# Three of four merged chunks turned by DMA transposes instead of by the matmul engine, in a hybrid attention and FFN layer

## The chip, the core and the metric

The kernel runs on one core of one Trainium2 chip. The core has a matmul engine (TensorE, PE in the profile), a vector engine (VectorE, DVE), an activation engine (ScalarE, ACT), a general engine (GpSimd, POOL) and a queue engine (SyncE, SP), and 16 DMA engines that move data for all of them. The metric is the device time of one execution in microseconds (us). The time before is the median of three runs, 1339.09 us (1338.78 to 1348.87).

## The reference

One layer on 256 rows of 2048 float32 values: a norm, one input projection, three kinds of attention, each projected and weighted with a gate, an output projection and a residual, then a norm, a gated feed-forward part and a residual. What the change touches is the line that merges the three branches and multiplies the sum with `w_out`:

```python
merged = (gates[:, :, 0] * (flat(o_a) @ w_branch[:ea])
          + gates[:, :, 1] * (flat(o_b) @ w_branch[ea:eb])
          + gates[:, :, 2] * (flat(o_c) @ w_branch[eb:]))
x = x + merged @ w_out

h2 = rmsnorm(x, g_ffn)
gu = h2 @ w_gu
x = x + (jax.nn.silu(gu[..., :D_FF]) * gu[..., D_FF:]) @ w_down
```

## The kernel before

The 256 rows are two tiles of 128 (`NT` = 2), and columns go in chunks of 512 (`NB`). Each float32 operand of a product is split into a high part of fewer bits and a rest: `split` (line 107) casts on ScalarE and subtracts on VectorE. A product of two such operands is three matmuls of 128x128 by 512 (lines 172 to 174). Weights come in blocks of 512 KB, two steps of k each (128 rows of the weight): `weights` (line 122) loads a block with a DMA of SP's queue into one of four `w_raw` buffers, casts it into one of five `w_hi` buffers and subtracts into one of five `w_lo`. `project` (line 147) runs over k for one chunk of output columns, with two tiles of rows, so that a block feeds 12 matmuls.

Work that is not a projection is written as generators in two lists, `stages` and `slow_stages`. `project` calls the first generator of `stages` once for each k but the first, and the first of `slow_stages` for each even k but the first: here a call is one step. A generator that ends is taken off, and the same call goes on with the next.

The order on an engine is set by a planner that simulates the kernel and takes what is ready, in program order as far as it can. `keep_in_program_order` pins an instruction behind the one written before it on the same engine; those written later can still be taken first. Buffers of a pool are given out as they come free.

The merge stage (lines 931 to 951): for each of four chunks, three projections with `w_branch` over 4, 6 and 6 steps of k give 3 + 5 + 5 = 13 calls of `stages`. Gates come back from memory with DMAs of POOL's queue (line 941) into buffers `sc` of 2 KB for each partition, of which there are 12 (`scratch`), and VectorE multiplies and adds (lines 945 to 948) into `ms`. The sum has rows on partitions, but the product with `w_out` needs it turned. So `to_m` (line 931) turns each half of a chunk (128 rows by 512 columns) with four TensorE transposes into PSUM (`transpose4`, line 201), and `m.put` splits them into `m_hi` and `m_lo`. One call of the generator does one half.

After that, `w_out` is projected in four chunks of columns over 16 steps of k (line 978), each of which reads all of m: chunk c of the merge is read at k = 4c to 4c + 3. `keep_x1` adds x, squares it and starts the next norm. `ph1` is the group of pools on the left side of the core's memory that holds the attention's output; it is closed at line 951, between the merge and the first `w_out` column, and the pools of the next stage are opened in its place.

In the feed-forward part `to_a` (line 1021) already turns 20 half chunks by DMA: a copy on ScalarE takes the two 16-bit halves of each float32 value apart into two planes (line 1034), a DMA transpose of ScalarE's queue turns the planes (line 1038), and another copy puts the halves together again (line 1047).

Of the kernel before, what the change touches and what calls it, by code (L numbers as in the profile page):

```python
# [11 lines left out]
U16 = mybir.dt.uint16  # L12
# [6 lines left out]
P = 128  # L19
D = 2048  # L20
S = 256
NT = S // P
KT = D // P
# [6 lines left out]
NB = 512  # L30
# [25 lines left out]
def hybrid_block(ctx: ExitStack, tc: tile.TileContext, x, w_in, w_branch, w_out, w_gu, w_down, rel_bias,  # L56
                 onehot, extra, across, factors, out):
    nc = tc.nc
# [22 lines left out]
    def pool(stack, name, side, bufs=1):  # L81
        return stack.enter_context(tc.tile_pool(name=name, bufs=bufs, side=side, reuse_waits="tile"))

    h2_stack, ph1, pm, pgx = ExitStack(), ExitStack(), ExitStack(), ExitStack()
# [6 lines left out]
    def half_kb(dt=F32):  # L91

        return scratch.tile([P, NB], dt, name="sc")
# [3 lines left out]
    def banks():  # L97

        turn.reverse()
        return [acc.tile([P, NB], F32, name=turn[1]) for _ in range(2)]  # L100
# [21 lines left out]
    def weights(w, row0, k0, nk, col0, there=()):  # L122

        for i, c in enumerate(range(k0, nk, 2)):
            raw = there[i] if i < len(there) else raw_weights(w, row0, c, col0)[0]
            hi = wpool.tile([P, 2, NB], F32R, name="w_hi")
            lo = wpool.tile([P, 2, NB], F32R, name="w_lo")
            split(hi, lo, raw)
            for k in range(2):
                yield c + k, hi[:, k, :], lo[:, k, :]  # L130


    stages, slow_stages = [], []

    def advance(queue):
        while queue:
            try:
                next(queue[0])
                return
            except StopIteration:  # L140
                queue.pop(0)

    def finish_stages(queue):
        while queue:
            advance(queue)

    def project(acts, k0, w, row0, nk, col0, ps=None, done=0, there=(), last=1):


        ps = ps or banks()  # L150
        held = []
        for k, w_hi, w_lo in weights(w, row0, done, nk, col0, there):
            if k:
                advance(stages)
            if k % 2 == 0 and k:
                advance(slow_stages)
            held.append((k, w_hi, w_lo))
            if k < nk - last or k == nk - 1:
                for t in range(NT):
                    for kk, hi, lo in held:  # L160
                        product(ps[t], *acts.plain(t, k0 + kk), hi, lo, kk == 0, kk == nk - 1)
                held = []
        return ps
# [5 lines left out]
    def product(ps, ah, al, wh, wl, start=False, stop=False):  # L169
        how = dict(skip_group_check=True)  # L170
        wh, wl = woven(wh), woven(wl)
        nc.tensor.matmul(ps, ah, wh, start=start, stop=False, **how)  # L172
        nc.tensor.matmul(ps, ah, wl, start=False, stop=False, **how)  # L173
        nc.tensor.matmul(ps, al, wh, start=False, stop=stop, **how)  # L174
# [26 lines left out]
    def transpose4(src):  # L201

        pt = tr.tile([P, 4, P], F32, name="tr")
        for i in range(4):
            nc.tensor.transpose(pt[:, i, :], src[:, i * P:(i + 1) * P], ident)  # L205
        return pt
# [127 lines left out]
    def begin_pair(acts, w, colA, colB):  # L334

        b11, b12 = (quarter(acts, w, 0, col0) for col0 in (colA, colB))
        p11 = [parts(b) for b in b11]
        u = [gx.tile([P, 2, NB], F32, name="u") for _ in acts.wc]
        for a, b, d in zip(b11, b12, u):
            nc.vector.tensor_add(d, a, b)  # L340
        b21 = quarter(acts, w, 1, colA)
        return p11, b12, u, b21, [parts(b) for b in (u if w is w_gu else b21)]
# [87 lines left out]
    h = Columns(p1, "h", KT)  # L430
# [7 lines left out]
    def load_x(c, queue):  # L438
        xc = [half_kb() for _ in range(NT)]
        for t in range(NT):  # L440
            queue(xc[t], x[t * P:(t + 1) * P, c * NB:(c + 1) * NB])
        return xc
# [408 lines left out]
    def gate_col(c, b):  # L851
        return 3 * NH * HD + b * D + c * NB

    def pair_of(kind, what):
        if kind == "qk":
            return hs, w_in, what * NB, NH * HD + what * NB
        if kind == "gates":
            return hs, w_in, gate_col(*what[0]), gate_col(*what[1])
        if kind == "vv":
            return hs, w_in, V0 + what[0] * NB, V0 + what[1] * NB  # L860
        if kind == "vg":
            return hs, w_in, V0 + what[0] * NB, gate_col(*what[1])
# [16 lines left out]
    for (kind, what), after in zip(units, units[1:] + [(None, None)]):  # L879
# [9 lines left out]
        if kind in ("qk", "gates", "vv", "vg"):  # L889
            ps, ahead = project_pair(*pair_of(kind, what), ahead, nxt, others is in_turn)  # L890
            if others is in_turn:
                turn.reverse()
        else:
            ps = project(h, 0, w_in, 0, KT, V0 + what * NB if kind == "v" else gate_col(*what),
                         *((ps0, 4, there) if (kind, what) == ("v", 0) else ()))
# [32 lines left out]
    tc.keep_in_program_order(nc.scalar.preload_act_table_set("natural_log_exp_and_others"))  # L928
    m = Columns(pool(pm, "pm", "right"), "m", KT)

    def to_m(c, srcs):
        for t in range(NT):
            m.put(c, t, transpose4(srcs[t]))
            yield

    for c in range(4):
        ms = [half_kb() for _ in range(NT)]
        for b, (k0, nk) in enumerate(((0, H_A), (H_A, H_B), (H_A + H_B, H_C))):
            gt = [half_kb() for _ in range(NT)]
            for t in range(NT):  # L940
                nc.gpsimd.dma_start(gt[t], gate_mem[b, c, t])
            ps = project(o, k0, w_branch, k0 * P, nk, c * NB)
            for t in range(NT):
                if b == 0:
                    nc.vector.tensor_mul(ms[t], ps[t], gt[t])
                else:
                    nc.vector.tensor_mul(gt[t], ps[t], gt[t])
                    nc.vector.tensor_add(ms[t], ms[t], gt[t])
        stages.append(to_m(c, ms))
    finish_stages(stages)  # L950
    ph1.close()


# [14 lines left out]
    def keep_x1(c, ps, xc):  # L968
        for t in range(NT):
            nc.vector.tensor_add(xc[t], ps[t], xc[t])  # L970
            nc.gpsimd.dma_start(x1[t, :, c * NB:(c + 1) * NB], xc[t])
        squares(xc, ss2, c)
        stages.append(next_h(c, xc))

    gx = pool(h2_stack, "gx2", "left", 2)
    for c in range(4):
        xc = load_x(c, nc.gpsimd.dma_start)
        ps = project(m, 0, w_out, 0, KT, c * NB)
        if c == 3:
            ahead = begin_pair(h2, w_gu, 0, D_FF)  # L980
        keep_x1(c, ps, xc)
# [301 lines left out]
```

## Time and profile before

| | us |
|---|---|
| median of three runs | 1339.09 |
| the profiled execution, first to last instruction (span) | 1337.6 |
| TensorE busy | 1331.3 |
| VectorE busy | 1154.7 |
| ScalarE busy | 927.8 |
| merge stage on TensorE, first product of a branch to first product with m | 514.9 to 600.4 |
| first `w_out` column on TensorE | 600.4 to 622.0 |

The span is what the profile shows of one execution; a run's time holds some more around it. Of TensorE the profile models the ends of the matmuls, which are pipelined, so that durations overlap and "busy" is not the same as "at its peak": the distance between starts is what counts. A row of the timeline gives start, duration, engine, line, operation, what is written and read, shapes and count, and in brackets the idle time before it with what ended it. PEclk is the TensorE clock that was granted, 1.00 being full speed. The DMA share is the mean busy share of the 16 DMA engines.

### The profile page before, as it was taken

To read this page: it belongs to the slowest core of one execution; us is meant where nothing else is said; L and a number is where in the kernel's file an instruction comes from. 1 tells how busy PE (TensorE), PEld (TensorE's weight loads), DVE (VectorE), ACT (ScalarE), POOL (GpSimd) and SP (SyncE) were. 2 spreads that over 40 slices of the span, in tenths; PEclk is the share of its full clock that TensorE was granted. 3 is DMA by queue.
4 is the path that set the end of the run, shared out by engine and by line. 5 is a ranking of instruction groups with operands and counts; after the bars stand their busy time and mean duration, and the time that the engine had idled before them with its cause. 6 is when DMAs were issued, how large, how long until landed. Compare 5 with 4: busy or idle time off the path is not lost.

```text
span 1337.6 us, 17737 instructions
## 1 busy us (share of the span) xinstructions
PE 1331.3 (100%) x6255; PEld 1161.6 (87%) x6255; DVE 1154.7 (86%) x1232; ACT 927.8 (69%) x1183; POOL 127.2 (10%) x191
## 2 busy tenths in 40 slices
PE   9999999999999999999999999999999999999998
PEld 6888888888888888888888888888888888888887
DVE  7978898988888897876689999998889997998887
ACT  6786967788777776445567787777877776665563
POOL 1100010001110112100100000001000001001010
PEclk9999999999999999999999999999999999999999
DMA  9987877888788878877797989889899987789993
GB/s 360 307 284 246 263 211 254 258 269 228 261 268 282 286 228 292 305 233 225 236 332 261 273 248 275 235 262 307 280 290 276 265 227 256 248 270 303 275 270 96
DMA packets 118929, 352.61 MB, mean 264 GB/s; under 512 B 32768, under 2 KB 34488, under 8 KB 118840
## 3 DMA queue, kind: packets, MB, share of 16 engines
q1 hardware_dynamic: 77016, 277.45, 58.4%
q0 software_dynamic: 19408, 67.66, 21.4%
q10 hardware_dynamic: 22416, 6.36, 3.2%
q8 instruction: 49, 0.80, 0.2%
q14 instruction: 40, 0.33, 0.1%
HBM read 294.26 MB, written 14.70 MB: 231 GB/s over the span
## 4 chain that ended last, share of the span: by engine, by line
PE 98%; DMA 1%; DVE 0%; SPq 0%; issue 0%; ACT 0%; DVEq 0%
PE qs L172 12%; PE qs L173 12%; PE qs L174 12%; PE ps L173 12%; PE ps L174 12%; PE ps L172 12%; PE z L172 4%; PE z L174 4%; PE z L173 4%; PE v L172 2%; PE v L174 2%; PE v L173 2%; PE tr L174 1%; PE tr L172 1%; PE tr L173 1%; PE tr L205 1%
## 5 line engine op out<-in xcount | busy, mean ns | idle before, releaser
L108 DVE TENSOR_TENSOR w_lo<-w_raw,w_hi 128x1024 fp32r<-128x1024 f32 x310 | 376.3, 1221 | 73.5 <-ACT w_hi L108 72.0
L108 ACT CAST w_hi<-w_raw 128x1024 fp32r<-128x1024 f32 x310 | 322.2, 1048 | 129.0 <-PE qs L174 52.8
L108 ACT CAST w_hi<-g_raw 128x1024 fp32r<-128x1024 f32 x208 | 214.4, 1050 | 103.6 <-DVE g_raw L329 32.1
L108 DVE TENSOR_TENSOR w_lo<-g_raw,w_hi 128x1024 fp32r<-128x1024 f32 x208 | 248.0, 1221 | 19.5 <-ACT w_hi L108 17.0
L108 ACT CAST w_hi<-u 128x1024 fp32r<-128x1024 f32 x156 | 162.6, 1048 | 107.0 <-PE ps L174 22.4
L108 DVE TENSOR_TENSOR w_lo<-u,w_hi 128x1024 fp32r<-128x1024 f32 x156 | 188.9, 1223 | 43.0 <-ACT w_hi L108 38.3
L173 PE MATMUL qs<-w_lo,h_hi 128*128 128x512 f32 x348 | 132.6, 381 | 0.0
L174 PE MATMUL qs<-w_hi,h_lo 128*128 128x512 f32 x348 | 132.1, 379 | 0.0
L173 PE MATMUL ps<-w_lo,h_hi 128*128 128x512 f32 x336 | 128.0, 381 | 0.3 <-DVE w_lo L108 0.2
L174 PE MATMUL ps<-w_hi,h_lo 128*128 128x512 f32 x336 | 127.4, 380 | 0.1
L172 PE MATMUL qs<-w_hi,h_hi 128*128 128x512 f32 x348 | 127.4, 382 | 0.0
L172 PE MATMUL ps<-w_hi,h_hi 128*128 128x512 f32 x336 | 123.0, 382 | 0.0
L172 PEld LDWEIGHTS qs<-w_hi,h_hi 128*128 128x128 f32 x348 | 65.7, 189 | 9.5 <-ACT sc L324 0.3
L174 PEld LDWEIGHTS qs<-w_hi,h_lo 128*128 128x128 f32 x348 | 65.8, 189 | 9.2
L173 PEld LDWEIGHTS qs<-w_lo,h_hi 128*128 128x128 f32 x348 | 65.8, 189 | 9.2
L388 POOL DMA_DIRECT2D u<-g_raw x44 | 38.3, 869 | 356.7 <-DVE w_lo L108 311.7
L173 PEld LDWEIGHTS ps<-w_lo,h_hi 128*128 128x128 f32 x336 | 63.5, 189 | 9.9 <-DVE w_lo L108 1.2
L174 PEld LDWEIGHTS ps<-w_hi,h_lo 128*128 128x128 f32 x336 | 63.5, 189 | 9.9 <-DVE h_lo L108 1.1
L172 PEld LDWEIGHTS ps<-w_hi,h_hi 128*128 128x128 f32 x336 | 63.3, 189 | 9.0 <-ACT h_hi L108 0.3
L340 DVE TENSOR_TENSOR u<-g_raw 128x1024 f32<-128x1024 f32 x44 | 53.6, 1221 | 11.7 <-DMA g_raw<-in_w_gu 11.0
L329 DVE TENSOR_TENSOR u<-u,g_raw 128x1024 f32<-128x1024 f32 x44 | 51.9, 1219 | 0.0
L172 PE MATMUL v<-w_hi,h_hi 128*128 128x512 f32 x104 | 39.5, 380 | 0.0
(407 smaller groups left out, 2945.8 us busy)
## 6 DMA issues: line engine op xcount, KB each, us to landing
w_raw<-in_w_in SPq DMA_DIRECT2D x103, 512.0 KB, 6.9
g_raw<-in_w_in SPq DMA_DIRECT2D x88, 512.0 KB, 6.3
g_raw<-in_w_gu SPq DMA_DIRECT2D x88, 512.0 KB, 6.0
w_raw<-in_w_gu SPq DMA_DIRECT2D x88, 512.0 KB, 6.6
w_raw<-in_w_down SPq DMA_DIRECT2D x56, 512.0 KB, 4.8
u<-g_raw POOLq DMA_DIRECT2D x48, 512.0 KB, 6.8
w_raw<-in_w_branch SPq DMA_DIRECT2D x32, 512.0 KB, 5.2
w_raw<-in_w_out SPq DMA_DIRECT2D x32, 512.0 KB, 4.3
```

Of the source, the lines that this page charges most:

```text
L108: cast, rest = nc.scalar.copy(hi, src), nc.vector.tensor_sub(lo, src, hi.bitcast(F32))
L172: nc.tensor.matmul(ps, ah, wh, start=start, stop=False, **how)
L173: nc.tensor.matmul(ps, ah, wl, start=False, stop=False, **how)
L174: nc.tensor.matmul(ps, al, wh, start=False, stop=stop, **how)
L205: nc.tensor.transpose(pt[:, i, :], src[:, i * P:(i + 1) * P], ident)
L329: tc.keep_in_program_order(nc.vector.tensor_add(d, d, a))
L340: nc.vector.tensor_add(d, a, b)
L388: nc.gpsimd.dma_start(d, a, accum_op=ALU.add)
```

## The change

Chunks 0, 1 and 2 of the merge are no longer turned on TensorE. The new `to_m` does with each half what `to_a` does: a copy on ScalarE into two 16-bit planes (`apart`), a DMA transpose on ScalarE's queue (`send`), and a copy that joins the planes in a scratch buffer (`join`), from which `m.put` splits as before. All three are pinned. Counted in calls of the generator, the halves are copied at call 2 and 6, sent at 3 and 7, and joined at 12 and 15; it has 15 calls for a chunk. The planes lie in a new pool of two buffers for each of the two tiles.

Chunk 3 is turned on TensorE as before, but from `slow_stages`, one half each at k = 4 and k = 6 of the first `w_out` column. That column, with its load of x, is now written ahead of `finish_stages` and the closing of `ph1`, because chunk 2's joins (k = 3 and 6 of this column) and chunk 3's transposes are called within it.

```diff
@@ -928,10 +928,45 @@
     m = Columns(pool(pm, "pm", "right"), "m", KT)
 
+    planes1 = pool(ph1, "planes1", "left", 2)
+
+    def apart(src):
+        halves = planes1.tile([P, 2, NB], U16, name="halves")
+        tc.keep_in_program_order(nc.scalar.copy(halves, src.bitcast(U16).rearrange("p (n h) -> p h n", h=2)))
+        return halves
+
+    def send(halves):
+        turned = planes1.tile([P, 8, P], U16, name="turned")
+        tc.keep_in_program_order(nc.scalar.dma_start_transpose(turned, halves.rearrange("p h n -> p (h n)")))
+        return turned
+
+    def join(turned):
+        st = half_kb()
+        tc.keep_in_program_order(nc.scalar.copy(
+            st.bitcast(U16).rearrange("p (k q h) -> p h k q", k=4, h=2),
+            turned.rearrange("p (h k) q -> p h k q", h=2)))
+        return st.rearrange("p (k q) -> p k q", k=4)
+
+    def steps(n):
+        for _ in range(n):
+            yield
+
     def to_m(c, srcs):
+        turned = []
         for t in range(NT):
+            yield from steps(2 * t + 1)
+            halves = apart(srcs[t])
+            yield
+            turned.append(send(halves))
+        yield from steps(5)
+        for t in range(NT):
+            m.put(c, t, join(turned[t]))
+            yield from steps(3 if t == 0 else 1)
+
+    def to_m_by_products(c, srcs):
+        for t in range(NT):
+            yield
             m.put(c, t, transpose4(srcs[t]))
-            yield
 
...
-        stages.append(to_m(c, ms))
+        if c < 3:
+            stages.append(to_m(c, ms))
+        else:
+            slow_stages.append(to_m_by_products(c, ms))
+    xc = load_x(0, nc.gpsimd.dma_start)
+    ps = project(m, 0, w_out, 0, KT, 0)
     finish_stages(stages)
+    finish_stages(slow_stages)
     ph1.close()
 
...
     for c in range(4):
-        xc = load_x(c, nc.gpsimd.dma_start)
-        ps = project(m, 0, w_out, 0, KT, c * NB)
+        if c:
+            xc = load_x(c, nc.gpsimd.dma_start)
+            ps = project(m, 0, w_out, 0, KT, c * NB)
```

## The prediction

> **What bounds the kernel now.** I read the page first (busy shares, the chain that ended last), then TensorE's waits, then the order of time around the merge stage (about 520 to 622 us), then the busy time in stretches of it.
>
> ```profile
> span 1337.6 us, 17737 instructions
> ...
> PE 1331.3 (100%) x6255; PEld 1161.6 (87%) x6255; DVE 1154.7 (86%) x1232; ACT 927.8 (69%) x1183; POOL 127.2 (10%) x191
> ...
> PE 98%; DMA 1%; DVE 0%; SPq 0%; issue 0%; ACT 0%; DVEq 0%
> ```
>
> ```profile
> PE tr L421 <- DVE sc L435: 1.1, 1, 1.1
> PE ps L526 <- DVE w_lo L520: 0.6, 1, 0.6
> PE ps L173 <- DVE w_lo L108: 0.2, 1, 0.2
> ```
>
> TensorE carries 98% of the chain that ended last. The second view gives who it waited for, with us in total, times and longest: 1.9 us in all, at three places. So the end moves only if TensorE gets less work, or if a new wait reaches it. The stage that the change touches, in stretches:
>
> ```profile
> core 0: us, PE busy (x) PEld busy (x) DVE busy (x) ACT busy (x) POOL busy (x), PEclk, DMA share, GB/s
> 541.00:550.00 9.00, 9.00 (x47) 7.95 (x46) 7.71 (x10) 4.23 (x5) 1.71 (x4) 1.00 0.94 330
> 550.00:562.00 12.00, 12.00 (x58) 10.50 (x57) 10.37 (x14) 5.25 (x5) 2.16 (x4) 1.00 0.85 275
> 562.00:574.00 12.00, 12.00 (x61) 10.59 (x60) 9.43 (x13) 5.46 (x7) 1.96 (x4) 1.00 0.85 276
> 574.00:585.00 11.00, 11.00 (x55) 9.61 (x54) 8.79 (x11) 4.84 (x5) 1.26 (x3) 1.00 0.82 261
> 585.00:594.00 9.00, 9.00 (x47) 7.95 (x45) 6.43 (x9) 4.47 (x6) 0.00 (x0) 1.00 0.73 220
> 594.00:610.00 16.00, 16.00 (x80) 14.07 (x79) 11.71 (x14) 7.08 (x8) 0.00 (x0) 1.00 0.67 199
> ```
>
> TensorE is busy all the time at a granted clock of 1.00; ScalarE is busy 31.3 of 69 us; the DMA share is 0.94 just where the first of the new transfers would fall, and 0.67 at the end.
>
> **Removed: 24 products on TensorE.** Chunks 0 to 2 lose eight transposes each. Their place in TensorE's order, the first and the last of the three groups:
>
> ```profile
> 541.01 0.38 PE L173 MATMUL qs<-w_lo,o_hi 128*128 128x512 f32 x1
> 541.22 0.38 PE L174 MATMUL qs<-w_hi,o_lo 128*128 128x512 f32 x1
> 541.44 1.04 PE L205 MATMUL tr<-ident,sc 128*128 128x128 f32 x8
> 542.23 0.46 PE L172 MATMUL qs<-w_hi,o_hi 128*128 128x512 f32 x1
> 542.53 0.38 PE L173 MATMUL qs<-w_lo,o_hi 128*128 128x512 f32 x1
> ...
> 584.63 1.04 PE L205 MATMUL tr<-ident,sc 128*128 128x128 f32 x8
> 585.42 0.46 PE L172 MATMUL qs<-w_hi,o_hi 128*128 128x512 f32 x1
> 585.72 0.38 PE L173 MATMUL qs<-w_lo,o_hi 128*128 128x512 f32 x1
> ```
>
> Durations overlap here, so I count from start to start. A product of 512 columns takes 0.215 us of the order (541.01 to 541.44 for two). From the first transpose to the second product behind it are 542.53 - 541.44 = 1.09 us, of which 0.215 is the product between: a group costs 0.875 us, and 585.72 - 584.63 gives the same. Three groups: 2.6 us. Nothing stands before or behind them as idle time, so all of it lies on the path.
>
> ```profile
> L205 PE MATMUL tr<-ident,sc x136: 272/273/328, 95.5 to 1121.6; 128*128 128x128 f32 x136
> ```
>
> One transpose lasts 273 ns by this row; by durations the sum would be 24 x 0.273 = 6.6 us, but eight of them lie inside 1.04 us, so starts decide. [...]
>
> **Added on ScalarE.** Per half chunk (six of them): a copy apart, the issue of a transpose, a copy that joins. The cast and the subtraction behind remain (they read the joined copy instead of PSUM). The same three operations run later in the kernel, on tiles of the same size:
>
> ```profile
> L1034 ACT COPY halves<-sc x20: 1040/1048/1056, 732.7 to 1083.3; 128x1024 uint16<-128x1024 uint16 x20
> L1038 ACTq DMA_TRANSPOSE turned<-halves x20: 1247/1622/4223, 733.7 to 1085.9; - x20
> L1047 ACT COPY sc<-turned x20: 1339/1347/1357, 753.8 to 1104.7; 128x1024 uint16<-128x1024 uint16 x20
> DMA to landing us min/median/max: 4.5/6.2/9.0
> ```
>
> Six times 1.05 + 1.62 + 1.35 is 24.1 us, into 37.7 idle us of ScalarE: it would be taken 55.4 of 69 us, or 80%. That lies near the stage that does this already:
>
> ```profile
> 700.00:1100.00 400.00, 400.00 (x1855) 350.07 (x1854) 369.18 (x346) 307.88 (x338) 28.93 (x36) 1.00 0.88 266
> ```
>
> There ScalarE is busy 307.9 and issues for 20 x 1.62 = 32 of 400 us (85%), VectorE is busy 92%, and TensorE still never stops. I take the added ScalarE work at nothing on the path. Its cover is the lead of the weight casts:
>
> ```profile
> 600.18 0.38 PE L174 MATMUL ps<-w_hi,o_lo 128*128 128x512 f32 x1
> 600.40 0.38 PE L172 MATMUL qs<-w_hi,m_hi 128*128 128x512 f32 x1
> 600.60 1.05 ACT L108 CAST w_hi<-w_raw 128x1024 fp32r<-128x1024 f32 x1 [1.54 <-PE ps L174]
> 602.63 1.22 DVE L108 TENSOR_TENSOR w_lo<-w_raw,w_hi 128x1024 fp32r<-128x1024 f32 x1
> ```
>
> The cast at 600.60 fills the buffer freed by the product at 600.18. With five buffers it belongs to the block that TensorE begins four blocks later: 600.40 + 4 x 12 x 0.215 = 610.7. Its second half is done at 603.85. The lead is 6.9 us. A wait on ScalarE under 6.9 us does not reach TensorE. Two copies and two issues in a row take 5.3 us at the median; with the longest issue twice, 10.5 us. The second is the bound on the bad side (a rival below); the good bound is no gain, as ScalarE is not on the path.
>
> What queues behind a new wait: a join that comes before its transfer has landed holds every later cast on ScalarE. A chunk's products give 3 + 5 + 5 = 13 steps, and the new stage takes 15 and a last call, so it begins two steps later with each chunk (the fifth step of chunk 3's products for chunk 2). The joins stand nine and eight steps behind their sends, at 6 x 0.215 = 1.29 us a step 11.6 and 10.3 us; the slowest landing seen is 9.0 us. The copies for chunk 0 can start when its sums are ready, about where its transposes stood (541.44).
>
> **The end of the stage.** m is first read at 600.40, so chunks 0 and 1 are far from late. For chunk 2 the last join is called at k = 6 of the first output column, and its columns are read from k = 8, about 610.7 us by the sum above. Its second send is called at k = 3 of chunk 3's last branch of six, which TensorE itself reaches at 600.40 - 3 x 1.29 = 596.5, and ScalarE, with its lead, before. With a landing of 9.0 us, 1.35 for the join, and for cast and subtraction
>
> ```profile
> L108 ACT CAST m_hi<-tr x8: 586/592/600, 542.1 to 607.3; 128x512 fp32r<-128x512 f32 x8
> L108 DVE TENSOR_TENSOR m_lo<-tr,m_hi x8: 681/682/684, 545.1 to 608.6; 128x512 fp32r<-128x512 f32 x8
> ```
>
> it needs 11.6 us and ends at 608.1 even from TensorE's own time, before 610.7. Chunk 3 keeps its eight transposes, now called at k = 4 and 6 of the first output column; they stood inside that column before, and TensorE went on behind them without a wait. That column's move ahead of the pools' change alters no operation: TensorE goes from 600.18 to 600.40 at its usual distance now, so no wait can be saved there. I price it at 0. A loss is bounded by the same rows, as the closed space is reused only by the norm of the next stage, which starts behind the column.
>
> **The queues.** SP's weight loads keep their order. POOL's gate loads wait for scratch buffers: one load stood behind the transposes, and will stand behind the copies apart.
>
> ```profile
> 542.34 1.07 POOL L941 DMA_DIRECT2D sc<-gate_mem  x2 [0.45 <-PE tr L205]
> 570.87 1.28 DVE L947 TENSOR_TENSOR sc<-ps,sc 128x512 f32<-128x512 f32 x2
> ```
>
> Counted in order this pair is the eighth, for chunk 2's second branch, read at 570.87: it may come 20 us later. The six joined tiles take scratch buffers for a few us each. Price 0.
>
> **The DMA engines.**
>
> ```profile
> q10 hardware_dynamic: 22416, 6.36, 3.2%
> ```
>
> ScalarE's queue holds 3.2% of 16 engines' span, 42.8 us, with some stores in it: a transpose takes at most 42.8 / 20 = 2.1 us of all engines, six 12.8 us. The stretches above leave free 0.54 + 1.8 + 1.8 + 1.98 + 2.43 + 5.28 = 13.8 us. Chunk 0's pair finds 0.54 free us for its 4.3: weights come up to 3.8 us later there, chunk 1's pair makes it 4.4 at most (1.9 left over, 4.3 more, 1.8 free), under the 6.9 us of lead. [...]
>
> **Sum.** The profiled execution: 1337.6 - 2.6 = 1335.0 us of span. The median of the runs is 1.5 us over this span (1339.09), so the forecast is 1336.5 us, 0.2% less. About 1%, 13 us, is what a measurement of this kernel can tell from no change.
>
> **Rivals.**
> (a) ScalarE's queue becomes the bound (slower). If a chunk's two copies and two issues stand in a row with issues of 4.2 us, casts are held 10.5 us and TensorE waits 10.5 - 6.9 = 3.6 us in each of three chunks: 10.8 less 2.6 is 8.2 us, 1347.3 us. It decides from a hold of 6.9 us, and loses the whole gain from 7.8 us. Against it: the stage at 700 to 1100, and free casts may be planned between. Chance 0.07.
> (b) The DMA engines become the bound. At twice the price 25.6 us stand against 13.8 free and 6.9 of lead: 4.9 us late, 1341.4 us. For it: 0.94 at 541 to 550. Chance 0.06.
> (c) The gain is there and is given back: the planner orders all instructions anew, and a wait of 2 to 3 us opens elsewhere. 1339.1 us. Chance 0.06.
> (d) A transpose's price is its duration, 273 ns: 1337.6 - 6.6 + 1.5 = 1332.5 us. Against it are the starts above. [...] Chance 0.03.
>
> **The numbers.** The forecast has 0.78. Its own range is 1335.5 to 1337.5 (bounds of the three groups, spread of the runs). The range from 1334.5 to 1341.5 takes in it, (b) and (c), 0.90 in all, less the tails of these. Faster by over 1% would need 13 us of TensorE's work, five times what is removed: 0.01. Slower by over 1% needs 16 us of waits, more than (a) at its bound: 0.02. Within 1%: 0.97.
>
> **What would show it.** Right: 24 fewer transposes between 540 and 590, six transposes on ScalarE's queue with landings of 4.5 to 9 us, TensorE without a wait from 520 to 622, the first product with m about 2.6 us earlier. Wrong: a wait of TensorE for w_hi or w_lo behind a chunk's copies (a), casts waiting for w_raw with a DMA share near 1 (b), or an unchanged merge stage start to end and a wait later on (c).

## The result, and the profile after

The changed kernel takes 1350.62 us (median of 22 runs, 1337.72 to 1357.23) against 1339.43 us for the kernel before (22 runs, 1338.68 to 1348.87). The ratio is 1.008, with a 95% interval from 1.0067 to 1.0094: slower by 0.8%, inside the 1% that the prediction called no change, but outside its range and on the other side. The profiled execution took 1355.23 us with a span of 1353.4 us, 15.8 more than the span before; it lies above the median, and so do the waits below. First the page of the changed kernel: span, engines, one DMA queue, the chain that ended last.

```profile
span 1353.4 us, 17704 instructions
...
PE 1334.1 (99%) x6231; PEld 1161.7 (86%) x6231; DVE 1153.8 (85%) x1232; ACT 939.7 (69%) x1195; POOL 127.2 (9%) x191
...
q10 hardware_dynamic: 28752, 7.93, 4.5%
...
PE 93%; DMA 4%; DVE 1%; ACT 1%; issue 1%; ACTq 0%; SPq 0%; DVEq 0%
```

TensorE has 24 instructions less, as it should. But DMA now carries 4% of the chain, where it had 1%. TensorE's waits in the changed kernel (engine, line and operand, releaser: us in total, times, longest):

```profile
PE qs L172 <- DVE sc L982: 6.7, 2, 6.4
PE ps L172 <- ACT w_hi L108: 3.2, 1, 3.2
PE ps L172 <- ACT m_hi L108: 1.9, 1, 1.9
PE ps L173 <- DVE w_lo L108: 1.2, 3, 0.8
PE tr L421 <- DVE sc L435: 1.1, 1, 1.1
PE ps L172 <- DVE sc L982: 0.9, 1, 0.9
```

The fifth is old, and two waits of the fourth, 0.4 us, stand before 562 us. The others add up to 13.5 us, all between 562 and 614 us. (The third names m_hi, but the product that waits there reads o_hi. Its PSUM buffer comes free with a multiplication of VectorE that stands behind a subtraction, and the cast ahead of that had stood 5.93 us for its block.) The stretches of the prediction, after (columns as there):

```profile
574.00:585.00 11.00, 6.89 (x31) 5.40 (x29) 4.23 (x6) 3.04 (x4) 1.08 (x2) 1.00 1.06 180
585.00:594.00 9.00, 7.04 (x22) 5.33 (x23) 6.65 (x8) 5.18 (x6) 0.82 (x2) 0.81 0.86 289
594.00:610.00 16.00, 13.55 (x63) 11.53 (x61) 5.95 (x7) 5.52 (x6) 0.79 (x2) 1.00 1.11 145
610.00:625.00 15.00, 11.02 (x45) 9.39 (x46) 12.99 (x17) 11.62 (x13) 0.00 (x0) 0.77 0.87 229
```

Read the last two columns together. From 574 to 585 the DMA engines were busy 0.82 and moved 261 GB/s before; now the share is 1.06 and 180 GB/s come through. More time in transfers, fewer bytes. (At 1.06 of 16 engines' time the times of packets overlap; how much of them is waiting, the share does not tell.) ScalarE is idler than before, 3.04 of 11 us against 4.84, so its queue is not full of work. What it waits for is in the chain of the changed kernel, in order of time (start, us, what):

```profile
566.31 2.52 ACTq L940
...
572.40 16.23 DMA w_raw<-in_w_branch
...
594.59 16.26 DMA w_raw<-in_w_out
610.93 1.05 ACT w_hi L108
...
613.15 0.69 DVE sc L982
613.98 0.77 PE qs L172
```

The first row is the issue of a transpose, which holds a cast back; issues make up 3.2 us of this chain from 535 to 625 us. Then two weight loads of 512 KB take 16 us each. The second ends at 610.9; the cast waits for it, the subtraction waits for the cast, the multiplication that frees a PSUM buffer stands behind that subtraction on VectorE, and TensorE stands until 613.98. So "DVE sc L982" in the list of waits is the last link, and a weight load the first. TensorE's timeline at that place:

```profile
607.17 0.38 PE L174 MATMUL ps<-w_hi,o_lo 128*128 128x512 f32 x1
613.98 0.77 PE L172 MATMUL qs<-w_hi,m_hi 128*128 128x512 f32 x1 [6.43 <-DVE sc L982]
614.54 0.63 PE L173 MATMUL qs<-w_lo,m_hi 128*128 128x512 f32 x1
614.97 0.63 PE L174 MATMUL qs<-w_hi,m_lo 128*128 128x512 f32 x1
...
617.53 0.63 PE L174 MATMUL qs<-w_hi,m_lo 128*128 128x512 f32 x1
617.95 0.55 PE L172 MATMUL qs<-w_hi,m_hi 128*128 128x512 f32 x1
```

Behind the wait the starts lie 0.43 us apart instead of 0.215, for some 4 us. What the distances exceed 0.215 by adds up to 2.2 us here and 2.1 us behind the wait of 3.2 us: 13.5 + 4.3 = 17.8 us of the 18.4 that are to be explained (15.8 more, although 2.6 were saved). Last, the DMA queues and issues of the changed kernel in 535 to 620 us (queue: packets, MB, share of 16 engines; issues: KB each, median us to landing), and the same view before:

```profile
DMA packets 11305, 19.19 MB, mean 226 GB/s; under 512 B 7012, under 2 KB 7012, under 8 KB 11301
...
q1 hardware_dynamic: 3685, 13.40, 56.0%
q10 hardware_dynamic: 6336, 1.57, 24.0%
...
w_raw<-in_w_out SPq DMA_DIRECT2D x8, 512.0 KB, 4.6
...
turned<-halves ACTq DMA_TRANSPOSE x6, 15.2
```

```profile
q1 hardware_dynamic: 4827, 17.54, 62.8%
...
w_raw<-in_w_out SPq DMA_DIRECT2D x15, 512.0 KB, 3.6
```

q10 is ScalarE's queue, here only the six transposes: 24.0% of 85 us of all engines is 20.4 us, 3.4 us each, any waiting included. q1 is SP's, the weights: 56.0% for 13.40 MB is 4.2% a MB, against 3.6% before, so a byte of weights is 17% dearer too. In 85 us, 8 blocks of `w_out` were issued instead of 15. The landings of the transposes, and below them of the weight blocks (each from the view of one tile, 530 to 625 us, changed kernel):

```profile
L940 ACTq DMA_TRANSPOSE turned<-halves x6: 1248/2519/6800, 540.7 to 599.3; - x6
...
DMA to landing us min/median/max: 10.2/15.2/18.3
```

```profile
DMA to landing us min/median/max: 3.6/6.4/17.2
```

### The profile page after: what moved, and what is told of

Read it like the earlier page. It is cut to its first block, busy times and chain, and to the rows that moved or that the text cites. A ratio compares the mean times of both kernels' runs of the same rounds, so it can differ in the third digit from the quotient of the medians.

```text
span 1353.4 us, 17704 instructions
## 1 busy us (share of the span) xinstructions
PE 1334.1 (99%) x6231; PEld 1161.7 (86%) x6231; DVE 1153.8 (85%) x1232; ACT 939.7 (69%) x1195; POOL 127.2 (9%) x191
## 4 chain that ended last, share of the span: by engine, by line
PE 93%; DMA 4%; DVE 1%; ACT 1%; issue 1%; ACTq 0%; SPq 0%; DVEq 0%
PE qs L172 12%; PE qs L174 12%; PE qs L173 12%; PE ps L173 11%; PE ps L174 11%; PE ps L172 11%; PE z L173 4%; PE z L174 4%; PE z L172 4%; PE v L172 2%; PE v L173 2%; PE v L174 2%; DMA w_raw<-in_w_branch 2%; DMA w_raw<-in_w_out 1%; PE tr L174 1%; PE tr L173 1%
```

## The experiments

Theory 1: transposes in flight slow the weight loads, these use up the lead of the casts, and TensorE stands. Its rivals: ScalarE's queue (copies, issues, or casts held behind joins), theory 2; transposes that collide with the gate loads of POOL's queue, theory 3; and the new order around the moved column, theory 4. All edits are to the changed kernel. "Before" is the kernel before, run on the same chip.

**The copies without the transfers, and the move alone.** The first leaves the transposes out and joins the planes as they are; the second turns all four chunks on TensorE and keeps the new order.

```diff
     def send(halves):
-        turned = planes1.tile([P, 8, P], U16, name="turned")
-        tc.keep_in_program_order(nc.scalar.dma_start_transpose(...))
-        return turned
+        return halves.rearrange("p h (k q) -> p (h k) q", q=P)
```

> The changed kernel without its six DMA transposes: the join reads the planes as the first copy left them, so the rows of chunks 0 to 2 of the merge are not turned and the output is another. All copies on ScalarE stay, the issues go. Theory 1 (transposes and weight loads in flight together slow each other, and weights come late): the waits go, 24 transposes of TensorE less, about 1336.5 us (1335.5 to 1338). Theory 2 (the added copies on ScalarE hold the weight casts): as slow as the changed kernel, 1345 us or more, with TensorE waiting for w_hi. Theory 3 (gate loads) says as theory 1. Theory 4 (the column's move) says as theory 2.

```diff
...
-        if c < 3:
-            stages.append(to_m(c, ms))
-        else:
-            slow_stages.append(to_m_by_products(c, ms))
+        (stages if c < 3 else slow_stages).append(to_m_by_products(c, ms))
```

> All four chunks turned by TensorE as before, but the first output column stands ahead of the closing of the pools, with chunk 3 turned from the slow stages. Theories 1, 2 and 3: as before, 1339 us within 1. Theory 4 (the move itself opens a wait at the first output column, where the changed kernel's longest one of 6.4 us stands): 1344 us or more.

Copies without transfers: 1336.99 us, 0.9978 (0.9969 to 0.9988) of before's 1339.61. That fits the 2.6 us of the removed products, with no price for twelve more copies on ScalarE. The move alone: 1339.19 us, 0.9997 (0.9983 to 1.001), nothing. The loss needs the transfers.

**Transfers whose result nobody reads.** The copies apart and the transposes stay; m comes from TensorE's transposes, and no join waits for a landing.

```diff
-            m.put(c, t, join(turned[t]))
+            m.put(c, t, transpose4(srcs[t]))
```

> The first copies and the six DMA transposes as in the changed kernel, but nobody reads what they write: m comes from TensorE's transposes, and there is no join. Theory 1: weight loads are late as in the changed kernel, and time is 2.6 us above it at most, 1345 to 1357 us. Theory 2 in its form of joins that wait for landings: no join waits, so about 1339 us, at most 1341.

1348.84 us (4 runs), 1.0066 (1.0046 to 1.0086). This kernel saves no products; it loses 9.2 us to before's 1339.61, where the changed kernel, its 2.6 us taken off, loses 1350.62 - 1339.43 + 2.6 = 13.8. Two thirds of the loss are there without a join, though with the issues on ScalarE. The rest may be joins that hold casts behind late landings (in the profile of the changed kernel one join waited, 3.3 us), or the spread of the runs; no run tells these apart. The landings of its transposes (the view of `turned`):

```profile
DMA to landing us min/median/max: 7.1/10.6/19.1
```

**Take the partners away.** Beside the transposes fly the gates (POOL's queue) and the weights (SP's). The first kernel leaves out the gate loads of chunks 1 to 3, the second the weight loads from chunk 1 to the first output column (one block is kept and used again).

```diff
-                nc.gpsimd.dma_start(gt[t], gate_mem[b, c, t])
+                if c == 0:
+                    nc.gpsimd.dma_start(gt[t], gate_mem[b, c, t])
+                else:
+                    nc.gpsimd.memset(gt[t], 1.0)
```

> The changed kernel, but the gates of chunks 1 to 3 are not loaded: GpSimd fills their buffers with ones, so the output is another. Theory 1 in its form of weight loads alone: transposes still land in 10 us and more, time 1343 to 1355 us. Theory 3 (the transposes collide with the loads of POOL's queue): landings as in the feed-forward part, 4 to 8 us, and about 1336.5 us.

```diff
+            if w is w_branch and col0 or w is w_out and not col0:
+                if not kept:
+                    kept.append(raw_weights(w, row0, c, col0)[0])
+                raw = kept[0]
...
```

> The changed kernel, but from chunk 1 of the merge to the first output column the weights are not loaded: every block is cast from one block that stays, so the output is another. The transposes have the gate loads of POOL's queue beside them and no weight loads. If weight loads in flight are what holds them, a pair is through in 3 to 6 us as in the feed-forward part, landings 4 to 8 us. If the gate loads alone hold them, landings stay at 10 us and more. TensorE waits for no weights either way, about 1336.5 us or less.

Without the gates: 1337.6 us, 0.9989 (0.9977 to 1.0001), three of ten runs near 1341.5. That fits neither theory 1 nor theory 3 as they were put. The transposes still landed after 6.1/9.8/12.0 us (shortest, median, longest) and the slowest weight block after 11.8 us, against 7.3 before and 17.2 in the changed kernel, so weights alone still hold the transposes. But most of the lost time is gone, and a MB of weights takes 3.6% of 85 us, as before the change. The row of SP's queue (535 to 620 us):

```profile
q1 hardware_dynamic: 4739, 17.25, 62.1%
```

In the profiled execution, the shortest of the ten, TensorE has no wait from 520 to 625 us. Without the weights: 1338.08 us in one run, which says little as a time; what counts is the landing of its transposes (the view of `turned`):

```profile
DMA to landing us min/median/max: 3.6/4.9/7.6
```

Beside the gates alone a transpose is as quick as in the feed-forward part (4.5/6.2/9.0). So the slow landings need the weights (15.2 us at the median with both, 9.8 without the gates, 4.9 without the weights), and most of the loss in time needs the gates as well (1337.6 us without them against 1350.62).

**How many, and on which queue.** One kernel turns only chunk 0 by DMA. Another issues the six transposes on SP's queue, among the weight loads. Two more put the gate loads on SP's queue, with the transposes on SP's and on ScalarE's.

```diff
...
-        if c < 3:
+        if c == 0:
             stages.append(to_m(c, ms))
         else:
-            slow_stages.append(to_m_by_products(c, ms))
+            (stages if c < 3 else slow_stages).append(to_m_by_products(c, ms))
```

> Only chunk 0 is turned by DMA, chunks 1 to 3 by TensorE. The pair takes some 10 us in the changed kernel and its weights have the lead of a quiet stretch behind them. Theory 1 with a lead that one pair does not use up (a chunk costs nothing, several in a row do, as the lead does not come back between): 0.9 us less than before, 1338.5 (1337.5 to 1340). If each pair costs its share of the changed kernel's loss: (1350.6 + 2.6 - 1339.4) / 3 - 0.9, 1343 us.

```diff
-        tc.keep_in_program_order(nc.scalar.dma_start_transpose(...))
+        tc.keep_in_program_order(nc.sync.dma_start_transpose(...))
```

> The six transposes go on SP's queue, between the weight loads, instead of ScalarE's. Theory 1 (transposes and weight loads that are in flight together on two queues slow each other): in one queue they follow each other, a pair is through in 3 to 6 us, weights come at most 5 us late, which the lead covers, 1336.5 us (1335.5 to 1339). If sharing the engines at all is enough, whatever the queue, or if the gate loads are the partner: 1343 us or more.

```diff
-                nc.gpsimd.dma_start(gt[t], gate_mem[b, c, t])
+                nc.sync.dma_start(gt[t], gate_mem[b, c, t])
```

> Transposes and the gate loads of the merge stage both go on SP's queue, so that transposes, weights and gates follow each other in one queue. If queues in flight beside each other are what slows the transfers: landings and time as for the transposes on SP's queue or better, 1336.5 us (1335.5 to 1338). If a gate load that waits for its buffer holds the weights behind it: TensorE waits, 1341 us or more.

> The changed kernel with the transposes on ScalarE's queue as they were, but the gate loads of the merge stage on SP's queue instead of POOL's: the same bytes, with one queue less in flight beside the transposes. If a third queue is what makes the transfers collapse: about as without gate loads, 1336.5 to 1339 us. If it is the bytes of gates and weights that a slowed set of DMA engines cannot move in time: 1343 us or more.

| | us | of before (95%) | landing of a transpose | of a weight block |
|---|---|---|---|---|
| chunk 0 only | 1338.45 | 0.9993 (0.9984 to 1.0002) | 7.1/7.2/7.2 | 3.5/5.1/7.4 |
| transposes on SP | 1337.51 | 0.9982 (0.9972 to 0.9991) | 5.4/6.6/9.2 | 3.4/5.1/9.3 |
| transposes and gates on SP | 1337.45 | 0.9982 (0.9973 to 0.9992) | 3.3/3.5/7.9 | 3.5/4.8/8.6 |
| gates on SP, transposes on ScalarE's | 1349.34 | 1.007 (1.005 to 1.009) | 6.8/9.8/12.1 | 3.3/4.6/10.0 |

One pair does no harm that can be measured: TensorE has no wait in that stage, and 0.07% of 1339, 0.9 us, is what the one group of products is worth, though the interval takes in no change. Its pair also landed quickly, after 7.2 us, while 1.05 MB of weights and 0.48 MB on POOL's queue moved beside it (544 to 551 us, 294 GB/s in all); the first pair of the changed kernel, in the same place, took 10.2 and 11.1 us. So a transpose among weights and gates is not always slow. Moving the same six transposes to SP's queue takes 13 us off, and the last two rows differ in nothing but the transposes' queue, and with it the engine that issues them: 12 us. The DMA view of the kernel with the transposes on SP, 535 to 620 us:

```profile
DMA packets 12468, 23.43 MB, mean 276 GB/s; under 512 B 7145, under 2 KB 7145, under 8 KB 12462
...
w_raw<-in_w_out SPq DMA_DIRECT2D x15, 512.0 KB, 4.8
...
turned<-halves SPq DMA_TRANSPOSE x6, 6.6
```

276 GB/s instead of 226, all 15 blocks issued. Where only the gates moved to SP, weight blocks land after 10.0 us at most and gates after 9.5 at the median, and TensorE waits behind the multiplications and sums of L982 and L983. Two rows of that kernel's DMA view, then of its list of waits, then what ScalarE and VectorE waited for ahead of work on `w_raw` (us, times):

```profile
sc<-gate_mem SPq DMA_DIRECT2D x16, 256.0 KB, 9.5
...
turned<-halves ACTq DMA_TRANSPOSE x6, 9.8
```

```profile
PE qs L172 <- DVE sc L982: 4.5, 2, 2.4
PE tr L205 <- DVE sc L983: 1.6, 1, 1.6
```

```profile
  DMA w_raw<-in_w_branch: 13.8, 6
  issue: 8.5, 3
...
  DMA w_raw<-in_w_out: 1.9, 1
```

The second row of the last view is casts that stood behind the issue of a transpose on ScalarE, 5.2 us at the longest. In the kernel with the transposes alone on SP no cast stands behind an issue, casts wait 18.0 us for weight blocks, more than the 15.7 here, and nothing is lost. So in these two profiles late weights alone do not explain the loss of the kernel with only the gates on SP; the held casts are the likelier link. No run changes the issuing engine and leaves the order of the transfers, so what the queue does to the transfers and what the issues do to ScalarE stay unseparated in these 12 to 13 us. The kernel with six on SP sends the last of them at 588.7 us and lands it within 9.2, long before the first one of `to_a` on ScalarE's queue (732.5 us in that kernel), so it shows nothing of transposes in flight on two queues at once.

**Is it the turning, or any traffic on a second queue?** Two kernels replace the transposes with plain copies of the same bytes on ScalarE's queue, once in rows of 2 KB, once with a gap behind each 256 B, so that a packet is as small as a transpose's. They leave the turning out.

```diff
-        tc.keep_in_program_order(nc.scalar.dma_start_transpose(...))
+        tc.keep_in_program_order(nc.scalar.dma_start(turned, halves.rearrange("p h (k q) -> p (h k) q", q=P)))
```

> The changed kernel with each transpose replaced by a plain copy on the same queue, of the same 256 KB from the same planes into the same tile, in rows of 2 KB; the rows of chunks 0 to 2 are not turned, so the output is another. If any transfer inside the core's memory on a second queue beside the weights collapses: 1343 us or more. If it is the transposes' kind of transfer (its 256-byte packets or the turning): landings under 6 us, 1337 us (1336 to 1339).

```diff
-        turned = planes1.tile([P, 8, P], U16, name="turned")
-        tc.keep_in_program_order(nc.scalar.dma_start_transpose(...))
+        turned = planes1.tile([P, 8, P + 14], U16, name="turned")
+        tc.keep_in_program_order(nc.scalar.dma_start(turned[:, :, :P], halves.rearrange("p h (k q) -> p (h k) q", q=P)))
...
```

> The same plain copies, but into tiles with a gap behind each 256 bytes, so that they go in packets of 256 bytes like those of the transposes; not turned, so the output is another. If the packets' size and number are what slows everything: landings of 10 us and more, 1343 us or more. If it is the turning itself: landings of 3 to 7 us, 1337 us (1336 to 1339).

Rows of 2 KB: 1336.79 us, 0.9977 (0.9968 to 0.9987). Packets of 256 B: 1337.28 us, 0.998 (0.997 to 0.9989). The DMA view of the second, 535 to 620 us:

```profile
DMA packets 12477, 23.87 MB, mean 281 GB/s; under 512 B 7047, under 2 KB 7047, under 8 KB 12471
...
q10 hardware_dynamic: 6240, 1.57, 8.3%
...
turned<-halves ACTq DMA_DIRECT2D x6, 256.0 KB, 8.0
```

As many small packets and as many bytes on the same queue as the transposes (6336, 1.57 MB), but 8.3% instead of 24.0% of the engines' time, and 281 GB/s instead of 226. (Without weights beside them the transposes took 12.1%.) The landings missed what was expected: 6.6/7.5/8.6 us for the rows of 2 KB and 6.9/8.0/11.2 for the small packets, no shorter than those of the transposes on SP. But the weight blocks beside them landed after 7.4 and 8.2 us at most. So neither bytes nor packet size nor a second queue as such is the cause. What is left is the turning, with the longer issue that comes with it (1.25 us and more against 0.47 to 0.70).

**A better version?** With the transposes on SP's queue TensorE has one new wait, 1.3 us, for chunk 3's sums. One more call before chunk 3's transposes should take it away.

```diff
     def to_m_by_products(c, srcs):
+        yield
         for t in range(NT):
```

> Transposes on SP's queue, and chunk 3's transposes on TensorE one step of the slow stages later (k = 6 and 8 of the first output column). With the transposes on SP's queue TensorE waited 1.3 us there, for chunk 3's sums. If that wait only stood in a place too early, it goes, and the time is 1.3 us below that kernel, 1336.2 us (1335.5 to 1337.5). If the sums are as much later: no difference, 1337.5 us.

1337.72 us (12 runs), 0.998 (0.997 to 0.9989). The wait is gone from its profile, but the median is no better than 1337.51 without the edit. Neither case fits, and 1.3 us is less than those ten runs spread (1336.12 to 1338.76). The best that was found is the transposes on SP's queue: 0.2% under the kernel before, 1337.5 us.

## Why the prediction was wrong

**Right.** 24 products are worth 2.6 us by their starts: 1339.61 to 1336.99 with copies alone. Rival (d), 6.6 us, would have shown as 1332.5. ScalarE's 24 us cost nothing as far as they are copies (copies alone), and the moved column nothing (the move alone). Of the issues the price was low: 2.5 us at the median and 6.8 at the longest against 1.62. Rival (a) as it was put, a hold of more than 6.9 us, did not come: casts stood 6.8 us behind issues in all three chunks together, 3.1 at the longest. In the stretch with the most lost time (574 to 585 us) ScalarE is less busy than before, 3.04 us against 4.84, and plain copies on its queue, with the same joins, cost nothing. But their issues are short, 0.47 to 0.70 us. The slow issues are a part of the loss, 3.2 us of the chain, and no run gives their size alone.

**The step that failed is "The DMA engines", and with it the landing that the joins were set against.** It took 2.1 us of all engines a transpose from the whole kernel's q10 row, and let the transposes fill the engines' idle time. Measured are 3.4 us, the mean of three unlike pairs (2.8, 7.7 and 10.0 us a pair). As a price without company 2.1 was not too low: without the weights the six took 12.1% of 85 us, 1.7 us each. The size alone would not have turned the result either: six at 3.4 are 20.4 us against the 13.8 free, 6.6 us late, still under the lead of 6.9. What failed is the form of the sum. The transfers did not just add up: beside weights and gates the transposes got slower and the weights with them, and the total fell to 145 GB/s (594 to 610 us) at a share above 1, where 199 had flowed before. A landing took 10.2/15.2/18.3 us where "9.0 at most" was taken as the bound, so a join stood 3.3 us for one, and weight blocks took up to 17.2 us, so a cast waited 10.3 us, beyond its lead:

```profile
610.93 1.04 ACT L108 CAST w_hi<-w_raw 128x1024 fp32r<-128x1024 f32 x1 [10.29 <-DMA w_raw<-in_w_out]
```

The 9.0 came from a stage with other traffic, and the trace before said so. The DMA view of a pair of transposes in the feed-forward part of the kernel before (737 to 743 us), and of a pair in the merge stage of the changed kernel (596 to 616 us):

```profile
q10 hardware_dynamic: 2086, 0.52, 65.1%
q0 software_dynamic: 158, 0.59, 49.2%
q1 hardware_dynamic: 43, 0.14, 6.8%
```

```profile
q10 hardware_dynamic: 2109, 0.52, 49.9%
q1 hardware_dynamic: 606, 2.22, 38.1%
q0 software_dynamic: 171, 0.53, 24.0%
```

In the feed-forward part a pair takes 65.1% of 6 us, 3.9 us, beside 0.14 MB of weights (23 GB/s) and 0.59 MB of POOL's queue (q0). The other nine pairs there, about 38.9 us apart, are alike in the weights: 0.06 to 0.25 MB in the same 6 us. In the merge stage this pair, the slowest, takes 49.9% of 20 us, 10 us, beside 2.22 MB (111 GB/s) and 0.53 MB. A row from a stage that does the same thing was used as a bound, without the traffic beside it.

**Rival (b)** had the engine, the place and the sign, at a chance of 0.06 and a price of 4.9 us. The measured price is 17.8 us of waits and slow restarts in the profiled execution, and 13.8 us by the medians. (b) missed the same thing: it doubled a price and kept the sum.

**The end of the stage and the queues.** m was ready; the first product with m came at 613.98 instead of 600.40 - 2.6 = 597.8 because weights and the VectorE work behind them were late. The gates, on POOL's queue, landed after 5.2 us at the median, far inside the 20 us that they were given to spare.

**Open.** Why transposes on one queue slow another queue's loads (17.2 us at the longest), and why on the loads' own queue they do so far less (9.3, against 7.3 before): the runs show that the turning, the weights, for most of the loss the gates, and ScalarE as queue and issuer are needed, but not the mechanism. Nor are these enough: the single pair of chunk 0 had them all and was quick. The changed kernel's runs spread over 20 us, and the lowest, 1337.72, shows hardly a loss; what decides in one execution was not found. Holding the weight loads back while transposes on ScalarE's queue fly was not tried.

## What to carry to other kernels

A transfer's price read in one stage did not hold beside other traffic here (landings of 4.5/6.2/9.0 us in the feed-forward part, 10.2/15.2/18.3 in the merge stage): look up what else is in flight there (the DMA view of just those us) before it is used elsewhere. Free share of the DMA engines was no budget to be filled here: with six transposes on ScalarE's queue the share went from 0.78 to 1.01 over 535 to 620 us, and 226 GB/s were moved instead of 255. A share above 1 with falling GB/s is a warning but no proof; in the feed-forward pair above the three queues add up to 121%, and TensorE does not stop (busy 6.00 of 6 us). Where DMA transposes must fly among weight loads, try them on the loads' own queue, which also takes the issues off ScalarE, and compare the landings (here 6.6 us at the median instead of 15.2).

## What the runs showed of the hardware

- Six DMA transposes of 256 KB on ScalarE's queue beside 512 KB loads on SP's and gate loads on POOL's: total down from 255 to 226 GB/s over 85 us, landings 15.2 us at the median. On SP's queue: 276 GB/s, 6.6 us. Plain copies of as many bytes and as small packets on ScalarE's queue: 281 GB/s, 8.0 us.
- Issuing a transpose on ScalarE's queue took 1.25/2.52/6.80 us (shortest, median, longest) in the changed kernel, where landings were 15.2 us at the median, and 1.25/1.46/2.23 without the weights, where they were 4.9; issuing a plain copy of the same bytes took 0.47 to 0.70 us.
- After a wait of 3.2 us and after one of 6.4 us TensorE started matmuls 0.43 us apart instead of 0.215 for some 4 us; the granted clock was 0.81 and 0.77 in these stretches (585 to 594 and 610 to 625 us). After the wait of 1.9 us they were 0.215 apart again within 0.3 us, and the clock of that stretch (574 to 585 us) was 1.00. So each of the two longer waits cost about 2 us more than it lasted (2.1 and 2.2).
